# One PSUM tile for a row of filler matmuls instead of a new tile for each

## The chip, the cores and the metric

The kernel runs on one NeuronCore of a Trainium2 chip. Its time is the device time of one execution in microseconds (us). Names of engines as in the profile: PE is TensorE's matmul side and PEld its weight loads, DVE is VectorE, ACT is ScalarE, POOL is GpSimd, SP is SyncE, which issues the transfers here.

## The reference

A trunk of four residual layers over 256 tokens of width 1024. Each layer has a token mixer and then a SwiGLU feed-forward part, each behind an RMS norm. The mixers are RWKV-7 (layers 0 and 3), stick-breaking attention (layer 1) and sparse attention over selected keys (layer 2). The beginning matters here: the RMS norm of x, and the first mixer.

```python
def rms_norm(x, g):
    y = x * lax.rsqrt(jnp.mean(x * x, axis=-1, keepdims=True) + RMS_EPS)
    return y * g

def rwkv7_time_mix(h, ...):
    shifted = jnp.pad(h, ((0, 0), (1, 0), (0, 0)))[:, :-1]
    xm = h[:, :, None, :] + (shifted - h)[:, :, None, :] * mix
    rkv = jnp.einsum('bsjd,jde->bsje', xm[:, :, :3], w_rkv)
    ...
    logw = -jax.nn.softplus(-(w0 + jnp.tanh(xw @ w1) @ w2)) - 0.5
    a = jax.nn.sigmoid(a0 + (xa @ a1) @ a2)
    ...

for i in range(4):
    h = rms_norm(x, norm_mix[i])
    x = x + mixer_i(h)
    x = x + swiglu(rms_norm(x, norm_ffn[i]), ffn_w_gu[i], ffn_w_down[i])
```

## The kernel before

Activations lie with the model dimension on the 128 partitions and the tokens along a row, so a matmul takes a 128x128 piece of a weight as stationary and 256 tokens as moving operand. Weights come from HBM in pieces of 128x1024 floats (tile `raw`, three buffers). ScalarE or VectorE rounds each into a first part (`wh`), VectorE subtracts to get the rest (`wl`), and TensorE multiplies both, which gives nearly the precision of float32 at a faster rate. A `raw` buffer is free for the next transfer when the VectorE instruction that writes its `wl` has read it; SP's queue is in order and waits for that.

The program is first recorded as a list of operations (class `Plan`) and then written out in an order that a table fixes (`ORDER`, packed in the source). The table says for each place which of the recorded operations stands there; a place with nothing (`None`) stands for fillers on TensorE. A place of fillers has two bf16 matmuls of 128x128 by 128x256 on a tile of ones, `warm_x`, whose result, `warm_o`, is never read. They go to a PSUM bank that no operation holds at that place: `emit` keeps in `held` for each of the six banks `ps_0` to `ps_5` the place of its last use and the buffer that still holds it, and takes the free bank that was used longest ago. The framework gives a wait to an instruction that writes a new tile in the place of an older one: it waits for the older one's last user, also where that is on the same engine. The order on each engine is that of the list; nothing reorders it.

There are 23 such places and so 46 filler matmuls: 38 in a row at the start of the program, four in a row at 153 us and two each at 1128 and 1130 us. From here on each of the 46 is called a filler.

What stands at the start, engine by engine:

- SP fetches x (`xt`, four tiles), the small vectors (`vecs`), the first part of the low-rank weights (`lora`) and the first `raw` pieces.
- ACT squares x (`sq`), VectorE adds the first three squares up in place; the fourth tile's two halves are squared on ACT and VectorE. Then PE sums over the partitions with a matrix of ones: `ss`, four matmuls, the first two on the sum of three squares and one each on the halves of the fourth. A float32 matmul shows as two records in the trace.
- From `ss` comes the norm's factor in six short operations: `rstda`, `rstd`, `rstda` on ACT and `rstdm`, `rstda`, `rstd` on VectorE. VectorE's `rstdm` is ordered behind ACT's first `rstda`.
- VectorE multiplies `lora` with the norm's weights and the mixing vectors in four pieces (`lora<-lora,mu`). PE multiplies these with x itself: `lora_in`, 16 matmuls, for which the norm's factor isn't needed. The first needs the first product, the second the second, the ninth and tenth the third and fourth.
- VectorE computes the normed x (`pre`) and the mixed inputs (`xm`), ACT and VectorE split them (`kx`), and PE multiplies them with the first `wh` and `wl`: `kp`, the first long row of matmuls.

On VectorE the order is: `sq`, `mu`, `sq`, four times `lora`, `rstdm`, `rstda`, `rstd`, `pre`, `wl`, and on to `kx`.

Of the kernel before, what the change touches and what calls it, by code (L numbers as in the profile page):

```python
# [15 lines left out]
F32 = mybir.dt.float32  # L16
# [8 lines left out]
P = 128  # L25
S = 256
# [193 lines left out]
WARMERS = 2  # L220
# [151 lines left out]
class Plan:  # L372
# [156 lines left out]
    def emit(self, nc, counts, warmer):  # L529
        def real(a):  # L530
            return a.real() if isinstance(a, View) else a

        ops = self.schedule()

        at = 0
        for tag in FIRST:
            b = next(b for b in sorted((b for b in self.bufs if b.slot == tag and b.ops), key=lambda b: min(self.place[o] for o in b.ops)))
            pad = (LEAD.get(tag, at % LINE) - at) % LINE
            if pad:
                b.pool.tile([P, pad // 4], F32, name=f"lead_{tag}")  # L540
            b.get()
            at += pad + 4 * b.width
        left = {b: set(b.ops) for b in self.bufs if b.group == "ps"}
        of, held = collections.defaultdict(list), {f"ps_{k}": (-1, None) for k in range(6)}
        for b in left:
            for o in b.ops:
                of[o].append(b)
        for n, o in enumerate(ops):
            if o is None:
                free = [(at, tag) for tag, (at, b) in held.items() if b is None]  # L550
                if free:
                    warmer(min(free)[1])
                continue
            for b in of[o]:
                left[b].discard(o)
                held[b.slot] = (n, b if left[b] else None)
            if not o.instrs:
                nc.scalar.preload_act_table_set(o.table)
            for method, args, kw in o.instrs:
                getattr(getattr(nc, o.eng), method)(*map(real, args), **{k: real(a) for k, a in kw.items()})  # L560
# [3 lines left out]
def trunk(ctx: ExitStack, tc: tile.TileContext, xT_in, vecs_in, wts, lora_in, consts_in, id32_in, outT, order, layers=None):  # L564
    nc = tc.nc
    ctx.enter_context(tc.manual_schedule())
    sb = ctx.enter_context(tc.tile_pool(name="sb", bufs=1))
    psum = ctx.enter_context(tc.tile_pool(name="psum", bufs=1, space=PSUM))
# [1027 lines left out]
    for k, (kind, i) in enumerate(subs):  # L1596
# [4 lines left out]
        else:  # L1601
            {"stick": stick, "dsa": dsa, "ffn": ffn}[kind](i, after)

    wx = sb.tile([P, S], BF16, name="warm_x")
    nc.vector.memset(wx, 1.0)
    plan.emit(nc, {"ps": 6, "g": 2, "xm": XMS, "raw": RAWS, "wh": 3, "wl": 3, "t": TS, "t2": 5},
              lambda tag: [nc.tensor.matmul(psum.tile([P, 512], F32, name="warm_o", tag=tag, bufs=1)[:, :S], wx[:, :P], wx, start=True, stop=True)  # L1607
                           for _ in range(WARMERS)])

# [123 lines left out]
def _build(nc, layers=None):  # L1735

    shapes = {"xT": (P, NC, S), "vecs": (P, len(VECS), NC), "wts": (_npieces(layers), P, PIECE), "lora": (2, P, NLORA),
              "consts": (P, NCONST), "id32": (P, 32, 32)}
    args = [nc.dram_tensor(f"in_{n}_dram", shapes[n], F32, kind="ExternalInput").ap() for n in _ARGS]
    args.append(nc.dram_tensor("out_0_dram", (P, NC, S), F32, kind="ExternalOutput").ap())  # L1740
    order = []
    with tile.TileContext(nc) as tc:
        trunk(tc, *args, order, layers=layers)
    assert len(order) == shapes["wts"][0]
    return order
# [25 lines left out]
```

## Time and profile before

| | |
|---|---|
| runs shown | 1365.06, 1365.79, 1367.98 us; median 1365.79 |
| profiled execution | 1365.3 us, of which the span is 1363.5 |
| busy share of the span | PE 99%, PEld 87%, DVE 83%, ACT 53%, POOL 1% |
| granted TensorE clock | 1.0 |
| DMA | 221.89 MB, mean 163 GB/s |
| the chain that ended last | PE 98%, DVE 1%, DMA 1% |

Start times in the profile are counted from the start of the span. A row of a timeline has the start, the length, the engine, the line and the operation with its tiles, and how many records were merged; in brackets stands how long the engine was idle before and what released it. Matmuls are pipelined, and a record holds a matmul's whole latency, so records that follow each other overlap: the distance of their starts is what one costs. A row of waits has who waited for whom, the total in us, how often, and the longest. A group of a tile's rows has the shortest, middle and longest record in ns. A row of windows has the stretch, then busy time and records of PE, PEld, DVE, ACT and POOL, the granted clock, the DMA's share and its GB/s.

### The profile page before, as it was taken

To read this page: it belongs to the slowest core of one execution; us is meant where nothing else is said; L and a number is where in the kernel's file an instruction comes from. 1 tells how busy PE (TensorE), PEld (TensorE's weight loads), DVE (VectorE), ACT (ScalarE), POOL (GpSimd) and SP (SyncE) were. 2 spreads that over 40 slices of the span, in tenths; PEclk is the share of its full clock that TensorE was granted. 3 is DMA by queue.
4 is the path that set the end of the run, shared out by engine and by line. 5 is a ranking of instruction groups with operands and counts; after the bars stand their busy time and mean duration, and the time that the engine had idled before them with its cause. 6 is when DMAs were issued, how large, how long until landed. Compare 5 with 4: busy or idle time off the path is not lost.

```text
span 1363.5 us, 25718 instructions
## 1 busy us (share of the span) xinstructions
PE 1353.9 (99%) x10380; PEld 1183.0 (87%) x10380; DVE 1131.2 (83%) x1913; ACT 728.2 (53%) x1245; POOL 8.3 (1%) x18
## 2 busy tenths in 40 slices
PE   9999999999999999999999999999999999999998
PEld 5888798888888898888899798888898888988888
DVE  5999799876688899876799989877699997998754
ACT  3765465654344655654346866554148564656532
POOL 0000000000000000000000000000000000000000
PEclk9999999999999999999999999999999999999999
DMA  5524157664655356655646546666653331666554
GB/s 181 169 88 126 34 154 219 200 194 145 186 175 165 113 185 202 203 176 163 199 155 184 157 140 216 204 196 203 187 153 111 111 98 34 199 206 199 174 172 132
DMA packets 62999, 221.89 MB, mean 163 GB/s; under 512 B 7328, under 2 KB 8864, under 8 KB 62624
## 3 DMA queue, kind: packets, MB, share of 16 engines
q1 hardware_dynamic: 62880, 220.25, 52.4%
q8 instruction: 81, 1.33, 0.4%
q14 instruction: 38, 0.31, 0.1%
HBM read 217.08 MB, written 1.05 MB: 160 GB/s over the span
## 4 chain that ended last, share of the span: by engine, by line
PE 98%; DVE 1%; DMA 1%; issue 0%; ACT 0%; DVEq 0%; SPq 0%
PE gate L560 18%; PE up L560 18%; PE dn L560 18%; PE po L560 7%; PE qk L560 6%; PE vp L560 4%; PE rp L560 3%; PE vps L560 3%; PE kp L560 3%; PE z L560 2%; PE warm_o L1607 1%; PE sc L560 1%; PE Y L560 1%; PE cmb L560 1%; PE pg L560 1%; PE attn_o L560 1%
## 5 line engine op out<-in xcount | busy, mean ns | idle before, releaser
L560 DVE TENSOR_TENSOR wl<-raw,wh 128x1024 fp32r<-128x1024 f32 x285 | 347.3, 1221 | 85.3 <-ACT wh L560 82.2
L560 ACT CAST wh<-raw 128x1024 fp32r<-128x1024 f32 x219 | 229.3, 1049 | 179.2 <-PE dn L560 92.4
L560 PE MATMUL dn<-h,wh 128*128 128x512 f32 (+1 forms) x726 | 244.3, 383 | 0.0
L560 PE MATMUL dn<-h,wl 128*128 128x256 f32 x704 | 198.1, 282 | 0.0
L560 PEld LDWEIGHTS dn<-h,wh 128*128 128x128 f32 x726 | 134.7, 188 | 26.9
L560 PE MATMUL up<-xg,wring 128*128 128x512 f32 x704 | 139.8, 336 | 0.0
L560 PE MATMUL gate<-xg,wring 128*128 128x512 f32 x704 | 138.3, 336 | 0.0
L560 PEld LDWEIGHTS dn<-h,wl 128*128 128x128 f32 x704 | 133.0, 189 | 0.0
L560 DVE TENSOR_TENSOR wring<-raw,wring 128x1024 fp32r<-128x1024 f32 x88 | 107.5, 1222 | 28.9 <-ACT wring L560 27.9
L560 PE MATMUL gate<-xg,wh 128*128 128x512 f32 x352 | 126.8, 392 | 0.0
L560 PE MATMUL up<-xg,wh 128*128 128x512 f32 x352 | 126.5, 392 | 0.0
L560 PEld LDWEIGHTS gate<-xg,wring 128*128 128x128 f32 x704 | 107.5, 188 | 14.7
L560 PEld LDWEIGHTS up<-xg,wring 128*128 128x128 f32 x704 | 107.4, 188 | 14.6
L560 ACT CAST wring<-raw 128x1024 fp32r<-128x1024 f32 x76 | 79.9, 1051 | 35.8 <-issue 15.3
L560 PE MATMUL up<-xg,wl 128*128 128x256 f32 x352 | 98.4, 280 | 0.0
L560 PE MATMUL gate<-xg,wl 128*128 128x256 f32 x352 | 98.4, 279 | 0.0
L560 PE MATMUL qk<-xg,wh 128*128 128x256 f32 (+1 forms) x384 | 91.8, 320 | 0.0
L560 PEld LDWEIGHTS up<-xg,wh 128*128 128x128 f32 x352 | 66.1, 188 | 14.5
L560 PEld LDWEIGHTS gate<-xg,wh 128*128 128x128 f32 x352 | 66.1, 188 | 14.5
L560 PE MATMUL qk<-xg,wl 128*128 128x256 f32 x256 | 71.7, 280 | 0.0
L560 PEld LDWEIGHTS qk<-xg,wh 128*128 128x128 f32 x384 | 63.8, 189 | 6.2 <-issue 0.5
L560 ACT COPY gus<-gate 128x256 f32<-128x256 f32 x88 | 32.3, 373 | 68.9 <-PE gate L560 66.8
(325 smaller groups left out, 2663.9 us busy)
## 6 DMA issues: line engine op xcount, KB each, us to landing
raw<-in_wts_dram SPq DMA_DIRECT2D x397, 512.0 KB, 3.8
lora<-in_lora_dram SPq DMA_DIRECT2D x2, 1536.0 KB, 9.0
rhl<-qa SPq DMA_DIRECT2D x32, 64.0 KB, 3.4
xt<-in_xT_dram SPq DMA_DIRECT2D x4, 256.0 KB, 3.6
lora<-in_lora_dram SPq DMA_DIRECT2D x2, 512.0 KB, 5.7
lg<-in_lora_dram SPq DMA_DIRECT2D x8, 128.0 KB, 3.6
inv<-in_id_dram SPq DMA_DIRECT2D x2, 512.0 KB, 4.0
out_dram<-xt SPq DMA_DIRECT2D x3, 256.0 KB, 4.5
```

What stands on the lines that cost most here:

```text
L560: getattr(getattr(nc, o.eng), method)(*map(real, args), **{k: real(a) for k, a in kw.items()})
L1607: lambda tag: [nc.tensor.matmul(psum.tile([P, 512], F32, name="warm_o", tag=tag, bufs=1)[:, :S], wx[:, :P], wx, start=True, stop=True) for ...
```

## The change

A filler takes a new PSUM tile only when there is none from the filler before, or when an operation has used that bank in between. Fillers in a row then write to one and the same tile, whether they come from one place or from several.

```diff
+        filler = None
         for n, o in enumerate(ops):
             if o is None:
                 free = [(at, tag) for tag, (at, b) in held.items() if b is None]
-                if free:
-                    warmer(min(free)[1])
+                if filler is None and free:
+                    filler = min(free)[1], warmer(min(free)[1])
+                if filler is not None:
+                    warmer(*filler)
                 continue
             for b in of[o]:
                 left[b].discard(o)
                 held[b.slot] = (n, b if left[b] else None)
+                if filler is not None and filler[0] == b.slot:
+                    filler = None
...
+    def warmer(tag, t=None):
+        if t is None:
+            return psum.tile([P, 512], F32, name="warm_o", tag=tag, bufs=1)
+        for _ in range(WARMERS):
+            nc.tensor.matmul(t[:, :S], wx[:, :P], wx, start=True, stop=True)
+
     plan.emit(nc, {"ps": 6, "g": 2, "xm": XMS, "raw": RAWS, "wh": 3, "wl": 3, "t": TS, "t2": 5},
-              lambda tag: [nc.tensor.matmul(psum.tile([P, 512], F32, name="warm_o", tag=tag, bufs=1)[:, :S], wx[:, :P], wx, start=True, stop=True)
-                           for _ in range(WARMERS)])
+              warmer)
```

On DVE, ACT, POOL and SP all instructions and waits are the same. On PE all instructions stand in the same order; what differs is waits of `warm_o` on a semaphore of PE itself (`PE_49`), 42 of them.

PE before, the end of the first row of fillers (`warm_o`) and the first `ss` and `lora_in`; the semaphores that an instruction waits for are in brackets:

```order
L1607 LDWEIGHTS warm_x
L1607 MATMUL warm_o<-warm_x 128x256 [waits PE_49]
L560 MATMUL ss<-sq,ones 128x256 [waits DVE_49,PE_49]
L560 MATMUL ss<-sq,ones 128x256
L560 MATMUL ss<-sq,ones 128x256 [waits Activation_49]
L560 MATMUL ss<-sq,ones 128x256 [waits DVE_49]
L560 MATMUL lora_in<-xt_99,lora 128x256 [waits DMAHW1_49,DVE_49]
L560 MATMUL lora_in<-xt_99,lora 128x256 [waits DVE_49]
```

And now:

```order
L1616 LDWEIGHTS warm_x
L1616 MATMUL warm_o<-warm_x 128x256
L565 MATMUL ss<-sq,ones 128x256 [waits DVE_49,PE_49]
L565 MATMUL ss<-sq,ones 128x256
L565 MATMUL ss<-sq,ones 128x256 [waits Activation_49]
L565 MATMUL ss<-sq,ones 128x256 [waits DVE_49]
L565 MATMUL lora_in<-xt_96,lora 128x256 [waits DMAHW1_49,DVE_49]
L565 MATMUL lora_in<-xt_96,lora 128x256 [waits DVE_49]
```

The filler's wait for PE is gone, as it is for the 36 fillers ahead of it (the very first had none); the first `ss` still waits for PE, since it takes the fillers' bank.

PE before, at 153 us, in the first RWKV mixer: the last two of four fillers and the small products behind them (`xu`):

```order
L1607 MATMUL warm_o<-warm_x 128x256 [waits PE_49]
L1607 LDWEIGHTS warm_x
L1607 MATMUL warm_o<-warm_x 128x256 [waits PE_49]
L560 MATMUL xu<-QC,XT 64x64 [waits PE_49,Activation_49]
L560 MATMUL xu<-QC,XT 64x64 x7
L560 MATMUL xu<-u_1841,XT 64x64 [waits DVE_49]
```

And now:

```order
L1616 MATMUL warm_o<-warm_x 128x256
L1616 LDWEIGHTS warm_x
L1616 MATMUL warm_o<-warm_x 128x256
L565 MATMUL xu<-QC,XT 64x64 [waits PE_49,Activation_49]
L565 MATMUL xu<-QC,XT 64x64 x7
L565 MATMUL xu<-u_1804,XT 64x64 [waits DVE_49]
```

Three waits are gone here, and one each at the two pairs of fillers after 1128 us; the first `xu` still waits for the last filler.

## The prediction

> **What bounds the kernel now.** I read the page's busy table and its chain first, then the waits of the first 40 us, then the timelines of that stretch engine by engine, and last the three later places where fillers stand.
>
> ```profile
> span 1363.5 us, 25718 instructions
> PE 1353.9 (99%) x10380; PEld 1183.0 (87%) x10380; DVE 1131.2 (83%) x1913; ACT 728.2 (53%) x1245; POOL 8.3 (1%) x18
> ...
> PE 98%; DVE 1%; DMA 1%; issue 0%; ACT 0%; DVEq 0%; SPq 0%
> ```
>
> TensorE carries 98% of the chain, so whatever lets its work begin earlier or run closer together should show in the end time. Some of that busy time is filler. The fillers as a group, then the matmuls of the first 30 us:
>
> ```profile
> L1607 PE MATMUL warm_o<-warm_x x46: 269/371/392, 1.2 to 1130.7; 128*128 128x256 bf16 x46
> ```
> ```profile
> 1.20 16.18 PE L1607 MATMUL warm_o<-warm_x 128*128 128x256 bf16 x38 [1.20 <-DVE warm_x L1605]
> 17.43 3.40 PE L560 MATMUL ss<-sq,ones 128*128 128x256 f32 x8
> 20.68 7.07 PE L560 MATMUL lora_in<-xt,lora 128*128 128x256 f32 x32
> 27.39 0.79 PE L560 MATMUL kp<-kx,wh 128*128 128x256 f32 x2
> ...
> 28.14 0.40 PE L560 MATMUL kp<-kx,wh 128*128 128x256 f32 x2
> ...
> 28.49 0.40 PE L560 MATMUL kp<-kx,wh 128*128 128x256 f32 x2
> ```
>
> The first 38 fillers take from 1.20 to 17.38 us. With the last one's record of 0.37 us taken off, 15.81 us over 37 steps is 0.427 us a step: a filler's whole latency (0.37 to 0.39) and some 0.04 more. The first real matmul, ss, starts at 17.43, behind them in TensorE's queue. Who waits in that time:
>
> ```profile
> PEld L1607 <- issue: 11.6, 36, 0.3
> ACT rstda L560 <- PE ss L560: 11.0, 1, 11.0
> DVE rstdm L560 <- ACT rstda L560: 8.9, 1, 8.9
> ...
> PEld ss L560 <- PE warm_o L1607: 0.7, 1, 0.7
> ```
>
> ss is released by the last filler; ScalarE sits 11.0 us and VectorE 8.9 us behind ss. Were the operands of ss there before? VectorE's rows, then ScalarE's:
>
> ```profile
> 6.12 0.69 DVE L560 TENSOR_TENSOR sq<-sq 128x512 f32<-128x512 f32 x1 [0.19 <-ACT sq L560]
> ...
> 8.93 0.42 DVE L560 TENSOR_TENSOR sq<-xt 128x256 f32<-128x256 f32 x1
> 9.95 2.51 DVE L560 TENSOR_TENSOR lora<-lora,mu 128x512 f32<-128x512 f32 x4 [0.60 <-DMA lora<-in_lora_dram]
> ...
> 21.38 0.42 DVE L560 TENSOR_SCALAR rstdm<-ss 128x256 f32<-128x256 f32 x1 [8.92 <-ACT rstda L560]
> 22.28 0.42 DVE L560 SCALAR_TENSOR_TENSOR rstda<-rstda,rstdm 128x256 f32<-128x256 f32 x1 [0.47 <-ACT rstda L560]
> ...
> 23.60 1.22 DVE L560 TENSOR_TENSOR wl<-raw,wh 128x1024 fp32r<-128x1024 f32 x1
> ...
> 27.34 0.41 DVE L560 TENSOR_TENSOR kx<-xm,kx 128x256 fp32r<-128x256 f32 x1
> ```
> ```profile
> 8.20 0.42 ACT L560 ACTIVATE sq<-xt 128x256 f32<-128x256 f32 x1 [2.11 <-DMA xt<-in_xT_dram]
> 8.63 1.28 ACT L558 ACT_TABLE_LOAD   x1
> 20.88 0.47 ACT L560 ACTIVATE rstda<-ss,eps_rms 128x256 f32<-128x256 f32 x1 [10.96 <-PE ss L560]
> ...
> 21.83 0.42 ACT L560 ACTIVATE rstda<-rstd 128x256 f32<-128x256 f32 x1
> 22.15 1.03 ACT L560 CAST wh<-raw 128x1024 fp32r<-128x1024 f32 x1
> ```
>
> They were. The first two ss instructions need the sum that is ready at 6.81, the third the square ready at 8.62, the fourth the one ready at 9.35. ss stands 8 us behind its data, held by fillers alone.
>
> **What a wait costs.** The change takes away 42 waits of a filler on the filler before it (37 at the start, then 3, 1 and 1), and adds, moves or removes no instruction. How close fillers then stand no row shows, so I bound it. Nearest are warm matmuls of the same 256 columns, each with a weight load: from 28.14 to 28.49 three kp matmuls start, 0.117 us each. But the array is not at full speed from the first:
>
> ```profile
> L560 PEld LDWEIGHTS ss<-sq,ones x8: 277/337/337, 17.4 to 20.2; 128*128 128x128 f32 x8
> L560 PE MATMUL ss<-sq,ones x8: 380/634/795, 17.4 to 20.5; 128*128 128x256 f32 x8
> ```
>
> The granted clock reads full throughout, yet ss steps by 0.41 us (17.43 to 20.68 for 8 records) and lora_in, of the same shape, by (7.07 - 0.38)/31 = 0.216. So ss ran at half speed until about its last two records (the shortest, 380 ns, is as short as lora_in's), some 2.9 us after dense work began, and 16 us of fillers a latency apart had not brought the array up. At half speed a dense filler takes about 0.234 us (twice 0.117). The 38 then end between 1.20 + 38 x 0.117 = 5.6 us (fast at once) and 1.20 + 38 x 0.234 = 10.1 (slow to the last). With full speed after 2.9 us, as for ss, 12 are slow and 26 fast: 7.1 us, the value I take.
>
> **The start, step by step.** ss one and two run at about 7.1, the third at 8.7, the fourth at 9.4, two records of 0.216 us each; ss ends near 9.85. ScalarE's table load ends at 9.91, and its three short operations (20.88 to 22.25 before, 1.37 us) run from 9.95 to 11.3. VectorE's queue has the four lora products in front of rstdm, and they end at 12.46 whatever TensorE does, because their DMA released them at 9.95. So rstdm starts near 12.4, and rstda 0.45 us later at 12.85, with no wait for ScalarE. Before it was 22.28: a shift of 9.4 us. What is late next is the lora product behind its DMA; ss has about 1.5 us of slack. All behind it on VectorE (rstd, pre, wl, kx) moves by the same 9.4 if the weights are there. The wl then stands at 14.2 and needs its wh cast; of the raw tiles three were issued early (engine busy times, then DMA share and GB/s):
>
> ```profile
> 10.00:12.00 2.00, 1.72 (x6) 0.53 (x5) 2.00 (x5) 0.00 (x0) 0.00 (x0) 1.00 0.81 332
> 12.00:14.00 2.00, 1.74 (x5) 0.42 (x4) 0.46 (x1) 0.00 (x0) 0.00 (x0) 1.00 0.07 27
> ...
> 22.00:24.00 2.00, 2.00 (x11) 1.77 (x10) 1.65 (x4) 2.00 (x3) 0.00 (x0) 1.00 0.00 0
> ```
>
> The transfers fall from 332 to 27 GB/s at about 12 us, so all three are in by 12.3 and the cast of 1.03 us ends by 13.4. SyncE's next loads are queued behind the release of these raw tiles by VectorE's wl; they start 9.4 us earlier too, and the DMA's rest (none moves at 22 to 24 us) only grows shorter. Nothing here hangs on a fixed time after 12.5 us.
>
> TensorE's own path: lora_in's first two instructions need the first two products, ready at about 10.6 and 11.25 (a quarter and half of the 2.51 us), and the remaining 15 instructions of two records take 15 x 0.43 = 6.5 us: 17.8. The second kp matmul needs kx, which ended at 27.75 and will end at 18.35. That leaves 0.6 us of slack, and kp moves by 9.4. From there TensorE is as full as before, and I carry 9.4 to the end.
>
> **The later fillers.** Pieces of the chain at 153 us and 1128 us:
>
> ```profile
> 153.51 0.28 PE warm_o L1607
> 153.79 0.04 issue
> 153.84 0.28 PE warm_o L1607
> ...
> 154.58 1.15 PE xu L560 x32
> ```
> ```profile
> 1128.75 0.28 PE warm_o L1607
> ...
> 1129.07 0.69 PE cmb L560 x32
> ```
>
> They lie on the chain, at full speed and 0.33 us apart; the work behind takes the fillers' bank and still waits for the last of them. Dense they stand 0.117 apart, which saves 0.21 us for each of 3 + 1 + 1 waits: 1.05. Ends: nothing, if another operand is late instead, and 1.05. Since xu follows the last filler and no other engine is named there, I take 0.9.
>
> **Sum.** 9.4 + 0.9 = 10.3 us. The profiled execution took 1365.3 us (span 1363.5 and 1.8 around it), 0.5 under the median of the three runs, 1365.79. 1365.3 - 10.3 = 1355.0 us.
>
> **Rivals.** *The array falls back to half speed* between the fillers' end and lora_in. From 7.1 to 11.2 us TensorE has only 5 x 0.43 = 2.2 us of work, about half, in pieces with pauses under 1 us. For it: the fillers of before were about half work too (0.234 of 0.427) and stayed slow. Against it: they show that such work does not bring the array up, not that it lets it down. Price: 3.4 us of lora_in at half speed (the length ss took, taken as the bound), 1.7 us lost, less 0.6 of slack; 1.1 of the gain gone: 1356.1. The Trainium skill, "TensorE: Matmul & The Clock Gate", section "A second HAM failure mode: psum-queue depth-cycling", tells of a clock that falls back from small pauses between groups of matmuls, which is this rival; no row here shows such a fall.
>
> *The fillers never reach full speed.* They end at 10.1, ss at half speed at 10.1 + 3.4 = 13.5, ScalarE at 14.95; rstda moves by 7.3 only: 1365.3 - 7.3 - 0.9 = 1357.1. Against it: dense ss came up in 2.9 us, and the fillers are dense for 8.9 if they stay slow. Part 1 of the same page says that the gate looks at freely running windows of about 3.4 us, so that the step may come up to one window late; by it the fillers end near 9.1, still inside the slack of ss, and this makes the rival less likely.
>
> *The fillers close up by half only*, because the wait before each weight load is put down to "issue" and not to a filler. At 0.27 us a step they end at 11.5, ss slow at 14.9, ScalarE at 16.35; rstda moves by 5.9, and half of the 0.9 comes: 1359.0. Against it: kp loads weights for each matmul and still steps by 0.117, and the fillers' step is a latency plus 0.04.
>
> *The start moves and the end does not*, since a later stage is paced by something else: about 1365. Against it: DMA has 1% of the chain.
>
> *Slower.* With denser fillers TensorE pauses longer in the later sparse stages and falls to half speed there; each fall costs 1.7 us. To lose 10.3 us and 2.7 more takes eight falls; the three later places give 5.1, which makes 1360.
>
> **Chances.** The sum 0.64; fallback 0.14; never fast 0.06; half closed 0.08; no move at the end 0.06; slower 0.02. About 0.2%, 2.7 us, is what a measurement can tell here from no change: faster 0.92, same 0.06, slower 0.02. The likeliest case alone runs from 1353.5 to 1356.0 (the runs before differ by 2.9 us, and which of them has the array up early is open); with fallback and slow fillers, 1352.5 to 1358.5 holds 8 in 10.
>
> **What would show it.** Right: fillers about 0.23, then 0.12 us apart and ended by 10; ss in short pieces between 7 and 10; VectorE's rstda at 12.9, right behind lora, its wait for ScalarE gone; the second kp matmul near 18.4; xu 0.6 us sooner after Y. Wrong: ss or lora_in records stepping by 0.43 us after 10 us, kp later than 19, a new wait for a raw tile before wl, or kp at 18 and an end that moved by much less than 9 us.

## The result, and the profile after

| | before | after |
|---|---|---|
| runs | 1365.06, 1365.79, 1367.98, 1368.37 us | 1353.65, 1354.03, 1354.46, 1357.93 us |
| median | 1366.88 us | 1354.24 us |
| profiled execution | 1365.3 us, span 1363.5 | 1357.93 us, span 1356.1 |
| mean granted clock of the profiled one | 1.0 | 0.996 |

The ratio of after to before is 0.9914, with a 95% interval of 0.9891 to 0.9937. The profiled execution of the changed kernel is the slowest of its four: the clock was half for some ten microseconds near 1117 us (shown below); the three others have a clock of 1.0 and lie between 1353.65 and 1354.46. The stretch before that is undisturbed and answers the prediction step by step.

The head of the page, then TensorE's first 19 us:

```profile
span 1356.1 us, 25718 instructions
PE 1347.7 (99%) x10380; PEld 1185.3 (87%) x10380; DVE 1131.6 (83%) x1913; ACT 729.2 (54%) x1245; POOL 8.4 (1%) x18
```
```profile
1.20 5.67 PE L1616 MATMUL warm_o<-warm_x 128*128 128x256 bf16 x38 [1.20 <-DVE warm_x L1610]
7.34 1.97 PE L565 MATMUL ss<-sq,ones 128*128 128x256 f32 x8 [0.47 <-DVE sq L565]
10.28 7.34 PE L565 MATMUL lora_in<-xt,lora 128*128 128x256 f32 x32 [0.97 <-DVE lora L565]
17.27 0.47 PE L565 MATMUL kp<-kx,wh 128*128 128x256 f32 x1
18.01 0.38 PE L565 MATMUL kp<-kx,wh 128*128 128x256 f32 x1 [0.27 <-DVE kx L565]
```

The row of fillers ends at 6.87 us instead of 17.38. What stands in brackets is the other half of the news: ss and lora_in were released by fillers and by ss before, and now wait for VectorE's data. The groups of the fillers and of ss in the first 40 us tell the speed:

```profile
L1616 PE MATMUL warm_o<-warm_x x38: 272/273/418, 1.2 to 6.6; 128*128 128x256 bf16 x38
```
```profile
L565 PEld LDWEIGHTS ss<-sq,ones x8: 187/190/190, 7.3 to 8.7; 128*128 128x128 f32 x8
L565 PE MATMUL ss<-sq,ones x8: 379/379/455, 7.3 to 8.9; 128*128 128x256 f32 x8
```

The longest filler record, 418 ns, is one at half speed and the middle one, 273, at full speed. ss, of which half the records took 634 ns or more, now has 379 as the middle, as lora_in had. VectorE's rows and the waits of the first 40 us:

```profile
9.54 2.51 DVE L565 TENSOR_TENSOR lora<-lora,mu 128x512 f32<-128x512 f32 x4 [1.51 <-DMA lora<-in_lora_dram]
...
11.96 0.42 DVE L565 TENSOR_SCALAR rstdm<-ss 128x256 f32<-128x256 f32 x1
12.48 0.43 DVE L565 SCALAR_TENSOR_TENSOR rstda<-rstda,rstdm 128x256 f32<-128x256 f32 x1
...
17.54 0.42 DVE L565 TENSOR_TENSOR kx<-xm,kx 128x256 fp32r<-128x256 f32 x1
```
```profile
PEld lora_in L565 <- DVE lora L565: 1.7, 2, 1.4
DVE lora L565 <- DMA lora<-in_lora_dram: 1.5, 1, 1.5
ACT rstda L565 <- PE ss L565: 1.3, 1, 1.3
```

ScalarE's wait for ss fell from 11.0 us to 1.3, and VectorE's 8.9 us behind rstda are gone: rstdm follows the lora products at once. rstda stands at 12.48 where it was at 22.28, and the second kp matmul starts at 18.01 where it was at 27.81. At the fillers of the first mixer the chain reads now:

```profile
142.82 0.56 PE warm_o L1616 x4
143.38 0.14 issue
143.51 1.15 PE xu L565 x32
```

The four fillers are one piece without "issue" between them, and only the last 0.14 us, the wait of xu, is left.

### The profile page after: what moved, and what is told of

Read it like the earlier page. It is cut to its first block, busy times and chain, and to the rows that moved or that the text cites. A ratio compares the mean times of both kernels' runs of the same rounds, so it can differ in the third digit from the quotient of the medians.

```text
span 1356.1 us, 25718 instructions
## 1 busy us (share of the span) xinstructions
PE 1347.7 (99%) x10380; PEld 1185.3 (87%) x10380; DVE 1131.6 (83%) x1913; ACT 729.2 (54%) x1245; POOL 8.4 (1%) x18
## 3 DMA queue, kind: packets, MB, share of 16 engines
HBM read 217.08 MB, written 1.05 MB: 161 GB/s over the span
## 4 chain that ended last, share of the span: by engine, by line
PE 98%; DVE 1%; DMA 0%; issue 0%; SPq 0%; ACT 0%; DVEq 0%
PE gate L565 18%; PE up L565 18%; PE dn L565 18%; PE po L565 7%; PE qk L565 6%; PE vp L565 4%; PE rp L565 3%; PE kp L565 3%; PE vps L565 3%; PE z L565 2%; PE sc L565 1%; PE cmb L565 1%; PE Y L565 1%; PE pg L565 1%; PE attn_o L565 1%; PE qi L565 1%
## 5 line engine op out<-in xcount | busy, mean ns | idle before, releaser
L565 ACT CAST wring<-raw 128x1024 fp32r<-128x1024 f32 x76 | 79.9, 1052 | 36.6 <-issue 12.3
```

## Experiments

All of them are timed beside the kernel before on the same chip. Where a run's mean granted clock is under 1.0, it is said, because one such fall costs more than most of the effects looked for. In the code cuts, `warmer` takes the number of its matmuls as a further argument.

**1 and 2: either half of the change alone.** A place of fillers is counted in `places`; the start has the first 19.

```diff
+                places += 1
+                if places > 19:          # experiment 1;  places <= 19 in experiment 2
+                    for _ in range(WARMERS):
+                        warmer(min(free)[1], warmer(min(free)[1]), 1)
+                    continue
```

The first row on one tile:

> The first row of 38 fillers shares one tile as in the changed kernel; the eight later fillers take a new tile each and wait, as before. Theory: the start gives nearly all. In the two traces TensorE is 10.4 us earlier at 27 us and the later places add 0.2 us for each of five waits, so this kernel should take 1.1 us more than the changed one: about 1355.1 where the changed one takes 1354.0 and the one before 1365.3. Rival (the later fillers carry more, for their waits lie on the chain at sparse places): 1357 or more.

The later fillers on one tile:

> The other half: the first row takes a new tile for each filler, only the eight later fillers share one. Theory: ss still starts at 17.4 us and only 5 x 0.21 = 1.05 us is gained, so about 1364.2 where the kernel before takes 1365.3. Rival: nothing (the gaps are filled by another wait), 1365.3. A fall of the clock at the later sparse place, if these shorter fillers cause it, would show here as 1368.

Experiment 1: ratio 0.9923 (0.991 to 0.9936), four runs of 1355.49 to 1358.06 us, of which the one with a clock of 1.0 took 1355.49. Experiment 2: 0.9985 (0.9975 to 0.9996), median 1364.5 of twelve runs, 1363.7 to 1365.1 in the ten with a clock of 1.0; the other two have 0.996 and took 1369.15 and 1369.37. So nearly all comes from the start and about 1 us from the later places, as the theory had it. The first line is TensorE's in experiment 1, the rest in experiment 2:

```profile
17.80 0.39 PE L572 MATMUL kp<-kx,wh 128*128 128x256 f32 x1 [0.27 <-DVE kx L572]
```
```profile
17.43 2.08 PE L572 MATMUL ss<-sq,ones 128*128 128x256 f32 x4
```
```profile
152.81 0.62 PE Y L572 x16
153.42 0.56 PE warm_o L1623 x4
153.98 0.14 issue
154.11 1.15 PE xu L572 x32
```

With the old first row ss stays at 17.43 us to the hundredth. Counted from the start of Y, xu comes after 1.30 us, where it came after 1.96 before (152.62 to 154.58): 0.66 us sooner. The last matmul of the program is 1.18 us sooner.

**3 and 4: how the queue is freed.** Is it the shared tile that counts, or only that TensorE's queue is free earlier? Experiment 3 leaves the first row out, experiment 4 keeps the first 8 of its 38 fillers with a tile and a wait each.

```diff
+                if places <= 19:         # experiment 3;  4 < places <= 19 in experiment 4
+                    continue
```

> The 38 fillers at the start are left out altogether; the later ones are as in the changed kernel. Theory that the fillers cost only by standing in the queue: ss starts near 7 us at half speed, takes 3.4 us, is done by 10.5 inside the slack behind the lora products, and has itself brought the array up by then; rstda on VectorE stays near 12.5 and the time is that of the changed kernel, 1354.0. Rival (a dense row is needed to bring the array up for lora_in): lora_in runs at half speed for up to 3.4 us, kp starts up to 1.1 us later, 1355.1.

> At the start only 8 of the 38 fillers, each with its new tile and its wait; the later ones are as in the changed kernel. They end at 1.2 + 8 x 0.427 = 4.6 us. Theory (what counts is when TensorE's queue is free, not how fillers get there): ss near 7 us and 1354.0 to 1355.1, as with no filler. Rival (the wait on its own engine costs in some other way, such as ss waiting for the bank): ss later than 9 us and 1356 or more.

Experiment 3: 0.9907 (0.9894 to 0.9919), 1354.22 to 1355.11 us, all four with a clock of 1.0: between its theory and its rival. Experiment 4: 0.9917 (0.9902 to 0.9932), median 1355.72 of five; 1354.04 to 1356.39 in the four with 1.0, two of them above the 1355.1 that the theory allowed. TensorE in 3 and in 4:

```profile
7.12 3.78 PE L572 MATMUL ss<-sq,ones 128*128 128x256 f32 x8 [7.12 <-DVE sq L572]
10.70 7.49 PE L572 MATMUL lora_in<-xt,lora 128*128 128x256 f32 x32
17.84 0.59 PE L572 MATMUL kp<-kx,wh 128*128 128x256 f32 x2
```
```profile
1.20 3.38 PE L1623 MATMUL warm_o<-warm_x 128*128 128x256 bf16 x8 [1.20 <-DVE warm_x L1617]
7.10 4.03 PE L572 MATMUL ss<-sq,ones 128*128 128x256 f32 x8 [2.52 <-DVE sq L572]
11.05 8.10 PE L572 MATMUL lora_in<-xt,lora 128*128 128x256 f32 x32
18.80 0.47 PE L572 MATMUL kp<-kx,wh 128*128 128x256 f32 x1
```

In both ss runs at half speed (3.78 and 4.03 us instead of 1.97), and still the first two kp matmuls end at 18.43 us in experiment 3, against 18.39 with the dense fillers. ss starts as soon as its data are there, with waiting fillers ahead of it or with none. What the changed kernel gains at the start is a queue that is free when the data come; sharing the tile is one way to it and leaving the fillers out another. In experiment 4 lora_in starts slow too and takes 0.76 us more than in the changed kernel, and the first two kp matmuls end at 19.39 us. Not all of that is the array's: the small vectors and the lora piece came late in that run, and VectorE's first lora product starts at 10.31 us, 0.77 later than in the changed kernel.

**5: more fillers.** Three matmuls in each of the first 19 places.

```diff
+                    warmer(*filler, 3 if places <= 19 else WARMERS)
```

> The changed kernel with 57 fillers in the first row instead of 38, all on one tile. At 0.109 us each, as measured there, the row ends about 2.1 us later, near 8.8 to 10 us. Theory (ss has slack behind the lora products, which end near 12 us whatever TensorE does): ss ends by 11, rstda on VectorE stays at 12.4 to 12.8 and the time is that of the changed kernel, 1354.0. Rival (the queue still sets the start): all 2.1 us come back, 1356.1.

Ratio 0.9929 (0.991 to 0.9948). Three of four runs had a clock under 1.0 and took up to 1359.33; the one with 1.0 took 1355.28, between the two expectations, so the times alone don't decide. Its span does: 1352.5 us, as the changed kernel's 1351.9 to 1352.7, with 2.8 us outside the span where the other kernels have 1.8. The trace says the same, TensorE first and then VectorE:

```profile
1.20 7.77 PE L1623 MATMUL warm_o<-warm_x 128*128 128x256 bf16 x57 [1.20 <-DVE warm_x L1617]
9.03 1.99 PE L572 MATMUL ss<-sq,ones 128*128 128x256 f32 x8
...
17.58 0.80 PE L572 MATMUL kp<-kx,wh 128*128 128x256 f32 x2
```
```profile
12.46 0.42 DVE L572 SCALAR_TENSOR_TENSOR rstda<-rstda,rstdm 128x256 f32<-128x256 f32 x1 [0.31 <-ACT rstda L572]
```

The row ends 2.1 us later and ss starts 1.7 us later than in the changed kernel; rstda stands at 12.46 against 12.48. It has just begun to wait for ScalarE again, by 0.31 us, and comes 3.15 us after VectorE's first lora product (9.31 us in this run) instead of 2.94: here the slack ends.

**6 and 7: no later fillers, and no fillers at all.** Each drops the places from 20 on, the second all places.

```diff
+                if places > 19:          # True in the kernel without any
+                    continue
```

> The changed kernel without its eight later fillers. Undisturbed it should gain what they still cost: 8 x 0.11 and the waits of the work behind for the last filler, 0.2 to 0.3 at three places, together 1.5 us: 1352.5 where the changed kernel has 1354.0. Theory (the later fillers help to hold the clock up in the sparse stages): more of its runs have a mean clock under 1.0 than the changed kernel's, and these take 1356 to 1358. Rival (they do nothing for the clock): as many as there, and a median near 1352.5.

> The dense first row alone, without the eight later fillers, once more, for how often its clock falls: none of five runs had fallen. Theory (the later fillers do not hold the clock up): at most a third of the runs under 1.0 and a median of 1353 to 1354. Rival (five lucky runs): half the runs under 1.0 and a median over 1355.

> No filler anywhere, 46 matmuls left out. Theory (the fillers only cost time here: at the start they hold up the queue, later they lie on the chain): the time of the kernel without the later fillers, 1353.0 in runs with a clock of 1.0, plus at most 0.5 for an ss at half speed. Rival (with no filler the clock falls more often, or lora_in runs slow): a median over 1354.5 and most runs with a clock under 1.0.

Without the later ones: 0.9902 (0.9886 to 0.9919), 1352.96 to 1354.56 us, five runs with a clock of 1.0; again 0.9904 (0.9888 to 0.9921), median 1353.27, two of four runs under 1.0 (1352.59 with 0.999, 1356.63 with 0.996). Without any: 0.9906 (0.9892 to 0.9921), 1352.67 to 1354.71, four runs of 1.0. These lie about 1 us under the changed kernel's 1353.65 to 1354.46, less than the 1.5 us expected, and their intervals overlap with its own; the profiled spans with a clock of 1.0 are 1351.3 us, 0.9 under the changed kernel's 1352.2. That the later fillers hold the clock up did not show in five runs; in the four more, two were under 1.0, which is over the third that was expected, while the median was as expected. The chain without later fillers, at the first mixer, and TensorE's start and VectorE's rstda without any:

```profile
142.53 0.62 PE Y L572 x16
143.15 1.08 PE xu L572 x32
```
```profile
10.85 8.27 PE L572 MATMUL lora_in<-xt,lora 128*128 128x256 f32 x32
18.76 0.59 PE L572 MATMUL kp<-kx,wh 128*128 128x256 f32 x2
```
```profile
12.49 0.42 DVE L572 SCALAR_TENSOR_TENSOR rstda<-rstda,rstdm 128x256 f32<-128x256 f32 x1 [0.47 <-ACT rstda L572]
```

xu follows Y directly. With no filler, lora_in runs slow at first and takes 8.27 us, and the first two kp matmuls end at 19.35 us, 0.96 later than in the changed kernel. The start is the same as in experiment 3, where they ended at 18.43: what differs is when the array came to full speed, 4.4 us after the start of ss there and 6.0 here. The span is still the same 1351.3 us as without the later ones alone. Matmul by matmul the kernel without any is 0.7 us behind that one at 153 us, 0.3 behind at 1115 and level from 1130: the loss was made up in several stages, and which waits took it in is not shown. The later fillers cost about a microsecond, and none showed a use in the times of these runs.

**8 and 9: where the clock falls.** The kernel before, for one more profile, and the changed kernel again.

> The kernel before, unchanged, for one more profile. About half of its runs have a mean clock of 0.998 and take 1366.8 to 1369, the others 1.0 and 1364.9 to 1367.8. Theory: a run with 0.998 shows a stretch of two windows of half clock, about 7 us, in the sparse stage near 1128 us, where the fillers stand. Rival: it stands at another place, so that the later fillers have nothing to do with it; or the profile shows a clock of 1.0 and tells only how late lora_in comes to full speed at the start.

> The changed kernel again, beside the kernel before on one chip, for more runs. Theory: 1353.7 to 1354.5 in runs with a clock of 1.0, 11.3 us under the fastest of the kernel before; in some runs the clock falls to half for three windows of a sparse stage, with 0.996 in the mean and 1357.5 to 1358. Rival (the first four runs were lucky): as many runs with a low clock as the kernel before has, about half.

The kernel before took 1370.43 us with a mean clock of 0.996, lower than the 0.998 expected. The changed kernel had a ratio of 0.9916 (0.99 to 0.9933) and a median of 1354.5; 1353.75 to 1354.34 in three runs of 1.0, 1354.66 with 0.999, and 1357.86 and 1358.35 with 0.996. So half of its six runs have a low clock, as the rival had it. Its profile, of a run with 1.0, has a span of 1352.2 us, 11.3 under the 1363.5 of the kernel before at 1.0. Windows of the kernel before in this run (the granted clock is the third number from the right), then single microseconds of the changed kernel's first profile, and its TensorE rows there:

```profile
1125.00:1130.00 5.00, 4.89 (x96) 3.19 (x91) 2.99 (x8) 0.37 (x1) 0.00 (x0) 0.86 0.00 0
1130.00:1135.00 5.00, 4.89 (x86) 4.00 (x88) 1.42 (x3) 0.89 (x3) 0.00 (x0) 0.50 0.02 3
1135.00:1140.00 5.00, 5.00 (x130) 4.75 (x130) 2.17 (x6) 0.98 (x3) 0.00 (x0) 0.62 0.01 3
```
```profile
1116.00:1117.00 1.00, 1.00 (x31) 0.89 (x28) 0.26 (x3) 0.37 (x1) 0.00 (x0) 0.87 0.00 0
1117.00:1118.00 1.00, 1.00 (x4) 0.34 (x3) 0.36 (x3) 0.00 (x0) 0.00 (x0) 0.50 0.00 0
...
1126.00:1127.00 1.00, 1.00 (x30) 1.00 (x32) 0.77 (x3) 0.38 (x1) 0.00 (x0) 0.51 0.06 16
1127.00:1128.00 1.00, 1.00 (x40) 1.00 (x36) 0.31 (x2) 0.20 (x1) 0.00 (x0) 1.00 0.00 0
```
```profile
1116.68 1.20 PE L565 MATMUL bn<-prhl,bonesr 128*128 128x512 f32 x2
1117.68 0.65 PE L1616 MATMUL warm_o<-warm_x 128*128 128x256 bf16 x2
```

The fall comes at the same place of the program in both. In the changed kernel it begins at about 1116.75 us (0.87 of the clock in that microsecond), in bn, ahead of the pair of fillers at 1117.68, and lasts until 1126.98. In the kernel before, the 0.86 means half clock for 1.4 us, so from about 1128.6, again in bn:

```profile
1128.27 0.98 PE L560 MATMUL bn<-prhl,bonesr 128*128 128x512 f32 x2
1129.05 0.86 PE L1607 MATMUL warm_o<-warm_x 128*128 128x256 bf16 x2
```

The profile of the second run without later fillers has the same fall, again of 10.2 us and again from bn on, here at about 1116.36 us, though no filler follows:

```profile
1116.08 0.99 PE L572 MATMUL bn<-prhl,bonesr 128*128 128x512 f32 x2
1117.00 1.06 PE L572 MATMUL cmb<-XT,zs 32*32 32x32 f32 x32
```
```profile
1116.00:1117.00 1.00, 1.00 (x14) 0.31 (x4) 0.49 (x2) 0.17 (x1) 0.00 (x0) 0.68 0.00 0
```

The fall is therefore not made by these fillers, close together or not. Runs with 0.998 and 0.999 have shorter falls by their mean clock; none of them was profiled, so where these lie is not shown. Over all experiments the clock was under 1.0 in 22 of 40 runs of kernels whose later fillers wait (the kernel before 19 of 36, experiment 1 3 of 4), in 10 of 35 with later fillers on one tile, and in 2 of 13 without later fillers. That the waiting ones make it fall more often is suggested by this and not shown: how often it falls differs from batch to batch, and no run changed the stretch ahead of bn.

## Why the prediction was right

- **Fillers.** 0.234 us a step at half speed and 0.117 at full speed were foreseen; the trace has 0.213 and 0.109, and full speed 2.8 us after the first filler (2.9 taken). The row ended at 6.87, against 7.1. That the moment of full speed, and with it the end of the row, came so close is luck. By the steps of single records, the same row of 38 came to full speed after 3.4 us in experiment 9, 4.4 in 6, 5.4 in 1 and 5.8 in the second profile of 6 (shown below), where it ended last, at 8.35. It did no harm: ss starts at 8.41 us there, inside its slack, and VectorE's rstda stands at 12.35. The rivals of fillers that never reach full speed or close up by half only are ruled out by the steps.

```profile
1.20 7.15 PE L1623 MATMUL warm_o<-warm_x 128*128 128x256 bf16 x38 [1.20 <-DVE warm_x L1617]
```

- **The new bound at the start.** As said, it is the lora product behind its DMA: rstdm follows it at once, and in experiment 5, with ss 1.7 us later, VectorE only just waits for ScalarE; 1.5 us of slack were foreseen. Two smaller readings were off. The raw tiles were not all in by 12.3 us: ScalarE waited 0.2 us for each of the three, the last time until 13.43, but VectorE's wl was not held up. And the second kp had 0.27 us of slack behind lora_in, not 0.6.
- **The shift there** was 9.8 us, not 9.4. The step was right and the release of its DMA moved: VectorE's first lora product starts at 9.54 us in this profile and at 9.95 in that of before; between 9.12 and 10.31 in the profiles of the experiments. So the term itself varies by about a microsecond from run to run.
- **A term left out.** The large `lora` transfer, for which TensorE waited 0.53 us at 36.89 before, was no longer waited for, and from there the changed kernel is 10.4 us ahead (before and after below). In experiment 1, 0.3 us of that wait were still there, and in the other profile of the kernel before (experiment 8) there was none at all. So these 0.6 us are a matter of the run and not the change's to keep.

```profile
36.89 0.45 PE L560 MATMUL lw<-tl,lora 64*128 64x256 f32 x1 [0.53 <-DMA lora<-in_lora_dram]
```
```profile
26.50 0.48 PE L565 MATMUL lw<-tl,lora 64*128 64x256 f32 x1
```

- **The later fillers** gave 1.18 us in experiment 2; 0.9 was taken and 1.05 set as the upper end. Matmul by matmul, 0.65 us come at the three waits at 153 us and 0.21 at each of the two pairs, together 1.07: all five waits came home, and the rest is scatter of the stages between.
- **The sum** for undisturbed runs is 9.8 + 0.6 + about 1 = 11.4 us, and the spans 1363.5 and 1352.2 differ by 11.3, against 10.3 foreseen. That they agree so well is in part chance, for the 1352.2 is of another run than the 9.8: in it the start gave 10.7, and TensorE then stood idle for 0.73 us at 146 us, where the profile shows nothing that it waited for. The time forecast was 1355.0 us and the median is 1354.24. The medians moved by 12.6, more than the undisturbed spans; the clock of the four runs of the kernel before is not on record, so whether falls made two of them slower is not known.
- **The rival of a fall between the fillers and lora_in** did not happen with the dense row. TensorE was idle for 0.47 us ahead of ss and 0.97 us ahead of lora_in, and lora_in still had 379 ns as its middle record and stepped by 0.216. The Trainium skill's page "TensorE: Matmul & The Clock Gate" tells of a clock that falls back from small pauses, in its section "A second HAM failure mode: psum-queue depth-cycling"; after the dense row, pauses of up to 0.98 us brought no such fall in any profile here. A half-speed lora_in was priced at 1.1 us; in the kernel with no filler, where the array was never up before, the first two kp matmuls end 0.96 us later.
- **The slower rival** named the right stage, with the wrong cause and price: the clock does fall in the later sparse stage, and one fall costs 3.9 us of span (1356.1 against 1352.2) where 1.7 was reckoned; but it also falls in the kernel before, ahead of the fillers, and with none of them.

## What to carry to other kernels

A new tile for a result that nobody reads is not free: each matmul then waits for the whole latency of the one before, here 0.427 us instead of 0.213 with the array at half speed, or 0.33 instead of 0.109 at full speed. Before filler work is put ahead of the first real instruction of an in-order queue, see when that instruction's data come and let the filler end before. And look which engine's row has the last release after the repair: here a transfer set the rest. Counted from VectorE's first lora product, which that transfer releases, rstda came 12.3 us later before; it came 2.94 us later with 38 dense fillers, 3.15 with 57 and 3.33 with none.

## What the runs showed of the hardware

- Sixteen microseconds of matmuls that kept the array at work about half of the time left it at half speed (fillers at 0.427 us a step from first to last, then ss at half speed). Dense ones brought it up, after 2.8 to 5.8 us in six profiles of such a row. Behind no filler or waiting ones it came up 2.9 us after the start of ss in one profile of the kernel before and 5.2 in the other, 4.4 in experiment 3, and about 6 in experiment 4 and in the kernel with no filler. So where full speed sets in differs by some 3 us between runs of one kernel.
- The page's granted clock reads 1.00 over this slow start; only the lengths and steps of the records show it. In the later fall the clock reads 0.50. The fall lasts 10.24 us in all five profiles that have it, of the kernel before, the changed one and experiments 4, 5 and 6, and it begins in the same pair of bn matmuls in all five.
- In the stage near 1117 us TensorE is busy in every microsecond by its records, with small matmuls of 32 and 64 columns and a few of 512 between, and the clock fell all the same, for about 10.2 us. Part 1 of the Trainium skill's page "TensorE: Matmul & The Clock Gate" puts the fall after an idle window of about 3.4 us; the length agrees with three such windows, while an idle window is not what the records show.
